# Layer end of a two-layer encoder: gate rows in other PSUM banks, x update on VectorE, mean square from scaled squares

## Chip, core and metric

The kernel runs on one core of a Trainium2 chip, in one launch. The metric is the device time of that launch in microseconds (us), the median of several runs. Five engines work side by side, each through its own list of instructions in order: TensorE (PE), VectorE (DVE), ScalarE (ACT), GpSimd (POOL) and SyncE (SP), which issues nearly all DMAs.

## The reference

Two encoder layers over 512 tokens of width 1024, in float32. Each layer normalises x, modulates it by the conditioning vector c, runs three token mixers side by side, merges them by sigmoid gates, projects, normalises again and adds the result to x:

```python
for l in range(DEPTH):                                   # DEPTH = 2
    mod = c_act @ w_ada[l] + b_ada[l]
    shift, scale, gate = split_cols(mod, (D, D, D))
    h = rms_norm(x, g_pre[l]) * (1.0 + scale) + shift
    ...                                                  # projections h @ w_in[l]
    o_a = (mla_branch(...) * silu(za)) @ w_o_mla[l]
    o_b = (swa_branch(...) * silu(zb)) @ w_o_swa[l]
    o_c = (diff_branch(...) * silu(zc)) @ w_o_diff[l]
    g = sigmoid(gcols)
    y = (g[0] * o_a + g[1] * o_b + g[2] * o_c) @ w_out[l]
    x = x + gate * rms_norm(y, g_post[l])

def rms_norm(x, g):
    return x * rsqrt(mean(x * x) + EPS) * g
```

The change concerns the last line and the rms_norm at the head of the next layer.

## The kernel before

Every float32 matmul is split in three: both operands are cut into a high part and a low part, and high x high, low x high and high x low are summed in PSUM (mm3, lines 87 to 89). A weight comes by DMA into one of two "wr" buffers, ScalarE makes the high part (L81), VectorE the low part (L84). The 512 tokens are four blocks of 128, t = 0 to 3.

Tiles are taken from pools by tag, each tag with a fixed number of buffers used in turn; a new tile waits until the last reader of the old one is done. PSUM has 8 banks of 128x512: "dn" has 2 (projections, merge outputs, out projection), "sc" 2 (attention scores), "tr" 2 (transposes), "pj" and "av" one each. In SBUF "tf" has 2 buffers, "x5" 2 (bias tiles of the attention; the profile names them x), "big" 8. A scheduler sets the order of each engine's instructions at build time from its own estimate of times; at run time each engine keeps that order.

A layer ends in three steps.

1. gate_rows (called in rest_of_layer, after the last gate projections and before the merge of the third mixer). The vector `gate` before its bias is a sum over the 128 partitions of acc; a matmul with ones sums and spreads it to all partitions (L292, L293). VectorE adds the bias row b_ada (L298) and multiplies by g_post (L299); both rows are loaded by DMAs issued in the same function (L295, L297). This is done for two halves of 512 columns. Then merge multiplies the third mixer by its weights, 8 output blocks of 12 matmuls in "dn" banks, each evicted by VectorE (L548).

2. out_phase. The first half of the out projection goes into four banks (acc4); its squares are summed by ScalarE (L1019) and it is multiplied by gg[0] (L1020). The second half is done token block by token block in "dn" banks: 24 matmuls, a Square with a sum (L1036), the sum of the two sums (L1038), the mean with epsilon (L307), the power -0.5 on GpSimd (L309), the multiply by gg[1] (L1041). x is loaded by SP (L1028), and the update is x + rs * y: in the first half of blocks 0 to 2 by two instructions of GpSimd (L1045, L1047), elsewhere by one of VectorE (L1049). SP stores the result (L1051).

3. Between the layers boundary_tok takes each updated block on: a Square of x with a sum on ScalarE (L315 in normed), mean (L307), power (L309), scaling (L317), eight transposes on TensorE (L371), modulation by four VectorE (L375) and four ScalarE (L379) instructions, and the split into hTh and hTl. The first projections of layer 1 (mla_in_step, "sc" banks for t = 0 and 1) read these.

Of the kernel before, what the change touches and what calls it, by code (L numbers as in the profile page):

```python
# [13 lines left out]
AF = mybir.ActivationFunctionType  # L14
ALU = mybir.AluOpType
AX = mybir.AxisListType

P = 128
S = 512
D = 1024  # L20
# [30 lines left out]
def hybrid_kernel(ctx, tc, x, c, w_ada, b_ada, g_pre, g_post, w_in, g_q, w_uq, g_kv, w_ukv,  # L51
# [16 lines left out]
    def stat(n):  # L68
        return T("st", [P, n], F32, 24)
# [3 lines left out]
    def Q(tag):  # L73
        count[0] += 1
        return ps.tile([P, S], F32, tag=tag, name=f"ps_{tag}_{count[0]}", bufs=PB[tag])
# [204 lines left out]
    def gate_rows(l):  # L280
        bg_step(100)
        acc = gate_acc[0]
        gg = []
        for hf in range(2):
            lo = hf * S
            g = T("x5", [P, 896])
            pg = Q("dn")
            ah = T("pt", [P, S], F32R)
            al = T("pt", [P, S], F32R)
            act_copy(ah, acc[:, lo:lo + S])  # L290
            sub(al, acc[:, lo:lo + S], f(ah))
            pe.matmul(pg, onesr, ah, start=True, stop=False)  # L292
            pe.matmul(pg, onesr, al, start=False, stop=True)  # L293
            bb = T("tf", [P, S])
            sp.dma_start(out=bb, in_=b_ada[l:l + 1, 2 * D + lo:2 * D + lo + S].broadcast_to([P, S]))  # L295
            gp = T("tf", [P, S])
            sp.dma_start(out=gp, in_=g_post[l:l + 1, lo:lo + S].broadcast_to([P, S]))  # L297
            dve.tensor_tensor(out=g[:, :S], in0=pg, in1=bb, op=ALU.add)  # L298
            dve.tensor_tensor(out=g[:, :S], in0=g[:, :S], in1=gp, op=ALU.mult)  # L299
            gg.append(g[:, :S])  # L300
        return gg

    def rms_cols(ssq, n, cols):
# [5 lines left out]
        pool.tensor_tensor(out=rs, in0=ms, in1=mhalf[:, 0:cols], op=ALU.pow)  # L309
        return rs  # L310

    def normed(xt):
        xn = T("big", [P, D])
        ssq = stat(1)
        act.activation(out=xn, in_=xt, func=AF.Square, accum_out=ssq)  # L315
        rs = rms_cols(ssq, [D], 1)
        dve.tensor_scalar(out=xn, in0=xt, scalar1=rs[:, 0:1], scalar2=None, op0=ALU.mult)  # L317
        return xn

# [684 lines left out]
    def out_phase(l, mm, gg, nhh, nhl):  # L1004
        us = out_half(l, 0, mm)
        acc = acc4(True)
        for k in range(KT):
            wh, wl = us[k // 2]
            cs_ = slice((k % 2) * S, (k % 2) * S + S)
            for t in range(NT):  # L1010
                ts_ = slice(t * P, (t + 1) * P)
                mm3(acc[t], mm[k][0][:, ts_], mm[k][1][:, ts_], wh[:, cs_], wl[:, cs_],
                    k == 0, k == KT - 1)
        ys = []
        for t in range(NT):
            y = T("zz", [P, S])
            ssq = stat(2)
            jk = T("tf", [P, S])
            act.activation(out=jk, in_=acc[t], func=AF.Square, accum_out=ssq[:, 0:1])  # L1019
            dve.tensor_tensor(out=y, in0=acc[t], in1=gg[0], op=ALU.mult)  # L1020
            ys.append((y, ssq))
        us = out_half(l, 1, mm)
        ws = list(mla_in_weights(l + 1)) if nhh is not None else None
        for t in range(NT):
            ts_ = slice(t * P, (t + 1) * P)
            y, ssq = ys[t]
            xt = T("big", [P, D])
            sp.dma_start(out=xt, in_=xin[l][t * P:(t + 1) * P, :])  # L1028
            a = Q("dn")
            for k in range(KT):  # L1030
                wh, wl = us[k // 2]
                cs_ = slice((k % 2) * S, (k % 2) * S + S)
                mm3(a, mm[k][0][:, ts_], mm[k][1][:, ts_], wh[:, cs_], wl[:, cs_],
                    k == 0, k == KT - 1)
            jk = T("tf", [P, S])
            act.activation(out=jk, in_=a, func=AF.Square, accum_out=ssq[:, 1:2])  # L1036
            tot = stat(1)
            dve.tensor_tensor(out=tot, in0=ssq[:, 0:1], in1=ssq[:, 1:2], op=ALU.add)  # L1038
            rs = rms_cols(tot, [D], 1)
            jk = T("tf", [P, S])  # L1040
            dve.tensor_tensor(out=jk, in0=a, in1=gg[1], op=ALU.mult)  # L1041
            for hf, yh in enumerate((y, jk)):
                xh = xt[:, hf * S:(hf + 1) * S]
                if hf == 0 and t < 3:
                    pool.tensor_scalar(out=yh, in0=yh, scalar1=rs, scalar2=1.0, op0=ALU.mult,  # L1045
                                       op1=ALU.mult)
                    pool.tensor_tensor(out=xh, in0=xh, in1=yh, op=ALU.add)  # L1047
                else:
                    dve.scalar_tensor_tensor(out=xh, in0=yh, scalar=rs, in1=xh, op0=ALU.mult,  # L1049
                                             op1=ALU.add)  # L1050
                sp.dma_start(out=xout[l][t * P:(t + 1) * P, hf * S:(hf + 1) * S], in_=xh)  # L1051
            if nhh is not None:
                ends = boundary_tok(l + 1, t, xt, nhh, nhl)
                if t == NT - 1:
                    fence[:] = ends
        return ws
# [142 lines left out]
```

## Time and profile before

| | |
|---|---|
| time, median of 3 runs | 1209.92 us (1208.97 to 1210.29) |
| the profiled execution, its own time | 1208.57 us |
| its span, first to last instruction | 1206.8 us |
| PE matmuls busy | 1165.8 us (97%) |
| DVE busy | 840.5 us (70%) |
| ACT busy | 632.2 us (52%) |
| POOL busy | 194.7 us (16%) |
| mean granted TensorE clock | 0.993 of full speed |

The profile is of one execution. Busy time is the time in which an engine had an instruction in work; matmuls are pipelined, so the next one starts before the one before it has ended, and their durations overlap. Idle time of the other engines costs nothing as long as TensorE does not wait for them. In a timeline the bracket behind an instruction gives the idle time of its engine ahead of it and what ended that; where an instruction waits for several things, the profile names the one that came last by its records. Times within the span are counted from its start.

### The profile page before, as it was taken

The numbers are of one execution on the slowest core, as the hardware profiler recorded it, in microseconds if no ns is written. First come the engines' busy times: TensorE is split into PE (matmuls) and PEld (weight loads), VectorE is DVE, ScalarE is ACT, GpSimd is POOL, SyncE is SP. The second block draws the span as 40 slices with busy tenths as digits, with TensorE's granted clock in tenths as the row PEclk, the third lists the DMA queues.
The fourth block names the chain that finished last, engine by engine and source line by source line (L and its number), as shares of the span: only waits on it lengthen the run. The fifth ranks groups of instructions, "written<-read, shape, count | busy, mean of one in ns | idle before, by whom it ended". The sixth has DMA issues, their size and how long they took to land.

```text
span 1206.8 us, 15578 instructions
## 1 busy us (share of the span) xinstructions
PE 1165.8 (97%) x5428; PEld 946.0 (78%) x5428; DVE 840.5 (70%) x1748; ACT 632.2 (52%) x1250; POOL 194.7 (16%) x238
## 2 busy tenths in 40 slices
PE   5799999999999999999999999999999999999997
PEld 4777788778887888887878888888888888888786
DVE  7854776988865687765557567678785468776553
ACT  5453565655543457654347456565554345665432
POOL 3410211111210010101141001122121001010123
PEclk9899999999999999999999999999999999999999
DMA  9638522356356333343454432324532432333442
GB/s 316 205 98 250 147 77 73 91 132 182 105 146 163 98 81 83 105 115 120 144 171 127 119 105 72 84 53 124 147 101 83 105 92 81 86 105 97 139 159 85
DMA packets 169523, 146.86 MB, mean 122 GB/s; under 512 B 7679, under 2 KB 146999, under 8 KB 169444
## 3 DMA queue, kind: packets, MB, share of 16 engines
q1 hardware_dynamic: 169316, 145.85, 41.9%
q8 instruction: 43, 0.70, 0.3%
q14 instruction: 36, 0.29, 0.1%
q0 software_dynamic: 128, 0.01, 0.0%
HBM read 135.83 MB, written 14.20 MB: 124 GB/s over the span
## 4 chain that ended last, share of the span: by engine, by line
PE 79%; DMA 7%; DVE 7%; issue 2%; POOL 2%; ACT 2%; SPq 1%; DVEq 0%; POOLq 0%; ACTq 0%
PE ps_dn L87 18%; PE ps_dn L89 18%; PE ps_dn L88 18%; PE ps_tr L691 5%; DMA wr<-in_w_in 3%; PE ps_sc L87 2%; PE ps_sc L89 2%; PE ps_sc L88 2%; PE ps_av L700 1%; PE ps_av L701 1%; PE ps_sc L939 1%; PE ps_sc L940 1%; DVE wl L84 1%; DMA wr<-in_w_ada 1%; PE ps_pj L87 1%
## 5 line engine op out<-in xcount | busy, mean ns | idle before, releaser
L87 PE MATMUL ps_dn<-hTh,wh 128*128 128x512 f32 x840 | 336.2, 400 | 1.7 <-ACT tf L479 1.1
L89 PE MATMUL ps_dn<-hTh,wl 128*128 128x512 f32 x840 | 334.5, 398 | 0.5 <-DVE wl L84 0.5
L88 PE MATMUL ps_dn<-hTl,wh 128*128 128x512 f32 x840 | 334.4, 398 | 0.0
L84 DVE TENSOR_TENSOR wl<-wr,wh 128x1024 fp32r<-128x1024 f32 x141 | 178.9, 1269 | 120.0 <-ACT wh L81 119.3
L81 ACT ACTIVATE wh<-wr 128x1024 fp32r<-128x1024 f32 x141 | 149.1, 1058 | 178.9 <-PE ps_dn L88 95.9
L87 PEld LDWEIGHTS ps_dn<-hTh,wh 128*128 128x128 f32 x840 | 158.1, 188 | 37.8 <-ACT tf L479 1.6
L89 PEld LDWEIGHTS ps_dn<-hTh,wl 128*128 128x128 f32 x840 | 157.9, 188 | 37.4 <-DVE wl L84 0.9
L88 PEld LDWEIGHTS ps_dn<-hTl,wh 128*128 128x128 f32 x840 | 158.0, 188 | 35.6
L84 DVE TENSOR_TENSOR pt<-ps_tr,pt 128x512 fp32r<-128x512 f32 x136 | 92.2, 684 | 35.2 <-ACT pt L81 34.4
L81 ACT ACTIVATE pt<-ps_tr 128x512 fp32r<-128x512 f32 x136 | 78.7, 596 | 70.8 <-PE ps_tr L691 69.5
L762 POOL TENSOR_SCALAR p<-p,st 128x512 f32<-128x512 f32 x64 | 48.6, 778 | 291.1 <-DVE st L760 237.6
L691 PE MATMUL ps_tr<-ident,p 128*128 128x128 f32 x544 | 93.0, 273 | 0.8 <-POOL p L762 0.8
L691 PEld LDWEIGHTS ps_tr<-ident,p 128*128 128x128 f32 x544 | 70.1, 141 | 20.7 <-POOL p L762 1.4
L87 PE MATMUL ps_dn<-u,wh 128*128 128x512 f32 x192 | 77.0, 401 | 1.3 <-DVE x L298 1.3
L950 POOL TENSOR_SCALAR ta<-ta,st 128x512 f32<-128x512 f32 x32 | 26.6, 833 | 313.9 <-DVE st L949 197.5
L89 PE MATMUL ps_dn<-u,wl 128*128 128x512 f32 x192 | 76.8, 400 | 0.0
L88 PE MATMUL ps_dn<-u,wh 128*128 128x512 f32 x192 | 76.1, 396 | 0.0
L881 POOL TENSOR_SCALAR p<-p,st 128x256 f32<-128x256 f32 (+1 forms) x64 | 41.4, 665 | 161.9 <-DVE st L879 116.0
L758 ACT ACTIVATE p<-ps_sc,st 128x512 f32<-128x512 f32 x64 | 43.7, 685 | 36.1 <-DVE st L757 35.9
L757 DVE TENSOR_REDUCE st<-ps_sc 128x1 f32<-128x512 f32 x64 | 43.3, 685 | 15.9 <-PE ps_sc L89 15.4
L873 ACT ACTIVATE p<-p,st 128x256 f32<-128x256 f32 (+1 forms) x64 | 35.6, 556 | 20.9 <-DVE st L871 20.2
L87 PEld LDWEIGHTS ps_dn<-u,wh 128*128 128x128 f32 x192 | 36.1, 188 | 10.4 <-DVE x L298 2.2
(345 smaller groups left out, 2105.0 us busy)
## 6 DMA issues: line engine op xcount, KB each, us to landing
wr<-in_w_in SPq DMA_DIRECT2D x105, 512.0 KB, 3.9
wr<-in_w_ada SPq DMA_DIRECT2D x32, 512.0 KB, 3.6
wr<-in_w_out SPq DMA_DIRECT2D x16, 512.0 KB, 3.7
big<-in_w_ada SPq DMA_DIRECT2D x10, 512.0 KB, 9.3
big<-in_x SPq DMA_DIRECT2D x8, 512.0 KB, 5.1
wr<-in_w_o_mla SPq DMA_DIRECT2D x8, 512.0 KB, 3.7
wr<-in_w_o_swa SPq DMA_DIRECT2D x8, 512.0 KB, 3.6
wr<-in_w_o_diff SPq DMA_DIRECT2D x8, 512.0 KB, 3.5
```

The lines of the kernel that those rows point to most:

```text
L81: return act.activation(out=out_, in_=in_, func=AF.Copy, scale=scale)
L84: return (eng or dve).tensor_tensor(out=out_, in0=a, in1=b, op=ALU.subtract)
L87: pe.matmul(o, ah, bh, start=start, stop=False)
L88: pe.matmul(o, ah, bl, start=False, stop=False)
L89: pe.matmul(o, al, bh, start=False, stop=stop)
L691: pe.transpose(tr[:, i * P:(i + 1) * P], b, ident)
L757: dve.tensor_reduce(out=nm[:, t:t + 1], in_=s, axis=AX.X, op=ALU.max, negate=True)
L758: act.activation(out=pr[:, t], in_=s, func=AF.Exp, bias=nm[:, t:t + 1], accum_out=sm[:, t:t + 1])
L762: pool.tensor_scalar(out=pr[:, t], in0=pr[:, t], scalar1=rr[:, t:t + 1], scalar2=1.0, op0=ALU.mult, op1=ALU.mult)
L873: act.activation(out=pr[:, i, :w], in_=pr[:, i, :w], func=AF.Exp, bias=nm[:, i:i + 1], accum_out=sm[:, i:i + 1])
L881: pool.tensor_scalar(out=pr[:, i, :w], in0=pr[:, i, :w], scalar1=rr[:, i:i + 1], scalar2=1.0, op0=ALU.mult, op1=ALU.mult)
L950: pool.tensor_scalar(out=pc[1], in0=pc[1], scalar1=rr[:, 1:2], scalar2=1.0, op0=ALU.mult, op1=ALU.mult)
```

## The change

In gate_rows the row sums go into "sc" banks instead of "dn" banks; the bias row is loaded straight into the tile that will hold the result, and both loads stand ahead of the matmuls in the code. In out_phase and normed the Square takes a scale of 1/sqrt(1024), so that its sum is the mean square; epsilon is added to the first half's mean right after it (L1027 of the changed kernel), and the sum of both halves is one instruction that reads this as a scalar (rms_of). The x update of all blocks and halves is on VectorE (L1052). rms_cols stays for the other norms.

```diff
--- before.py
+++ after.py
@@ -284,18 +284,18 @@
         for hf in range(2):
             lo = hf * S
             g = T("x5", [P, 896])
-            pg = Q("dn")
+            sp.dma_start(out=g[:, :S], in_=b_ada[l:l + 1, 2 * D + lo:2 * D + lo + S]
+                         .broadcast_to([P, S]))
+            gp = T("tf", [P, S])
+            sp.dma_start(out=gp, in_=g_post[l:l + 1, lo:lo + S].broadcast_to([P, S]))
+            pg = Q("sc")
             ah = T("pt", [P, S], F32R)
             al = T("pt", [P, S], F32R)
             act_copy(ah, acc[:, lo:lo + S])
             sub(al, acc[:, lo:lo + S], f(ah))
             pe.matmul(pg, onesr, ah, start=True, stop=False)
             pe.matmul(pg, onesr, al, start=False, stop=True)
-            bb = T("tf", [P, S])
-            sp.dma_start(out=bb, in_=b_ada[l:l + 1, 2 * D + lo:2 * D + lo + S].broadcast_to([P, S]))
-            gp = T("tf", [P, S])
-            sp.dma_start(out=gp, in_=g_post[l:l + 1, lo:lo + S].broadcast_to([P, S]))
-            dve.tensor_tensor(out=g[:, :S], in0=pg, in1=bb, op=ALU.add)
+            dve.tensor_tensor(out=g[:, :S], in0=pg, in1=g[:, :S], op=ALU.add)
             dve.tensor_tensor(out=g[:, :S], in0=g[:, :S], in1=gp, op=ALU.mult)
             gg.append(g[:, :S])
         return gg
@@ -309,11 +309,17 @@
         pool.tensor_tensor(out=rs, in0=ms, in1=mhalf[:, 0:cols], op=ALU.pow)
         return rs
 
+    def rms_of(ms, eps):
+        me, rs = stat(1), stat(1)
+        dve.tensor_scalar(out=me, in0=ms, scalar1=eps, scalar2=None, op0=ALU.add)
+        pool.tensor_tensor(out=rs, in0=me, in1=mhalf[:, 0:1], op=ALU.pow)
+        return rs
+
     def normed(xt):
         xn = T("big", [P, D])
-        ssq = stat(1)
-        act.activation(out=xn, in_=xt, func=AF.Square, accum_out=ssq)
-        rs = rms_cols(ssq, [D], 1)
+        ms = stat(1)
+        act.activation(out=xn, in_=xt, func=AF.Square, scale=D ** -0.5, accum_out=ms)
+        rs = rms_of(ms, EPS)
         dve.tensor_scalar(out=xn, in0=xt, scalar1=rs[:, 0:1], scalar2=None, op0=ALU.mult)
         return xn
 
@@ -1014,16 +1020,19 @@
         ys = []
         for t in range(NT):
             y = T("zz", [P, S])
-            ssq = stat(2)
+            ms = stat(2)
             jk = T("tf", [P, S])
-            act.activation(out=jk, in_=acc[t], func=AF.Square, accum_out=ssq[:, 0:1])
+            act.activation(out=jk, in_=acc[t], func=AF.Square, scale=D ** -0.5,
+                           accum_out=ms[:, 0:1])
+            dve.tensor_scalar(out=ms[:, 0:1], in0=ms[:, 0:1], scalar1=EPS, scalar2=None,
+                              op0=ALU.add)
             dve.tensor_tensor(out=y, in0=acc[t], in1=gg[0], op=ALU.mult)
-            ys.append((y, ssq))
+            ys.append((y, ms))
         us = out_half(l, 1, mm)
         ws = list(mla_in_weights(l + 1)) if nhh is not None else None
         for t in range(NT):
             ts_ = slice(t * P, (t + 1) * P)
-            y, ssq = ys[t]
+            y, ms = ys[t]
             xt = T("big", [P, D])
             sp.dma_start(out=xt, in_=xin[l][t * P:(t + 1) * P, :])
             a = Q("dn")
@@ -1033,21 +1042,15 @@
                 mm3(a, mm[k][0][:, ts_], mm[k][1][:, ts_], wh[:, cs_], wl[:, cs_],
                     k == 0, k == KT - 1)
             jk = T("tf", [P, S])
-            act.activation(out=jk, in_=a, func=AF.Square, accum_out=ssq[:, 1:2])
-            tot = stat(1)
-            dve.tensor_tensor(out=tot, in0=ssq[:, 0:1], in1=ssq[:, 1:2], op=ALU.add)
-            rs = rms_cols(tot, [D], 1)
+            act.activation(out=jk, in_=a, func=AF.Square, scale=D ** -0.5,
+                           accum_out=ms[:, 1:2])
+            rs = rms_of(ms[:, 1:2], ms[:, 0:1])
             jk = T("tf", [P, S])
             dve.tensor_tensor(out=jk, in0=a, in1=gg[1], op=ALU.mult)
             for hf, yh in enumerate((y, jk)):
                 xh = xt[:, hf * S:(hf + 1) * S]
-                if hf == 0 and t < 3:
-                    pool.tensor_scalar(out=yh, in0=yh, scalar1=rs, scalar2=1.0, op0=ALU.mult,
-                                       op1=ALU.mult)
-                    pool.tensor_tensor(out=xh, in0=xh, in1=yh, op=ALU.add)
-                else:
-                    dve.scalar_tensor_tensor(out=xh, in0=yh, scalar=rs, in1=xh, op0=ALU.mult,
-                                             op1=ALU.add)
+                dve.scalar_tensor_tensor(out=xh, in0=yh, scalar=rs, in1=xh, op0=ALU.mult,
+                                         op1=ALU.add)
                 sp.dma_start(out=xout[l][t * P:(t + 1) * P, hf * S:(hf + 1) * S], in_=xh)
             if nhh is not None:
                 ends = boundary_tok(l + 1, t, xt, nhh, nhl)
```

The instruction lists differ from those of before only at the layer ends. In the rows below a number behind a name tells tiles of one tag apart; lines below the first edit have moved by 3 to 9 (L548 is L554 now, L1041 is L1049).

VectorE in the gate rows of layer 0, x being the tiles of the two halves and wl the low parts of merge weights. Before:

```order
L298 TENSOR_TENSOR x_1186_5281<-ps_dn_5282,tf_5289 128x512
L84 TENSOR_TENSOR wl_5404<-wr_5402,wh_5403 128x1024
L299 TENSOR_TENSOR x_1186_5281<-x_1186_5281,tf_5291 128x512
L298 TENSOR_TENSOR x_1192_5295<-ps_dn_5296,tf_5303 128x512
L548 SCALAR_TENSOR_TENSOR p_5183<-p_5183,ps_dn_5317 128x512
L299 TENSOR_TENSOR x_1192_5295<-x_1192_5295,tf_5305 128x512
L548 SCALAR_TENSOR_TENSOR p_5183<-p_5183,ps_dn_5336 128x512
L553 SCALAR_TENSOR_TENSOR op_5316<-p_5183,op_5315 128x512
```

Now:

```order
L298 TENSOR_TENSOR x_1186_5281<-ps_sc_5285,x_1186_5281 128x512
L298 TENSOR_TENSOR x_1191_5294<-ps_sc_5298,x_1191_5294 128x512
L84 TENSOR_TENSOR wl_5402<-wr_5400,wh_5401 128x1024
L299 TENSOR_TENSOR x_1186_5281<-x_1186_5281,tf_5283 128x512
L299 TENSOR_TENSOR x_1191_5294<-x_1191_5294,tf_5296 128x512
L554 SCALAR_TENSOR_TENSOR p_5183<-p_5183,ps_dn_5315 128x512
L554 SCALAR_TENSOR_TENSOR p_5183<-p_5183,ps_dn_5334 128x512
L84 TENSOR_TENSOR wl_5446<-wr_5444,wh_5445 128x1024
```

The second L298 has come up from behind L299 to stand right after the first, ahead of the low part, and both L299 stand together; the two merge evictions (L548, now L554) follow each other.

VectorE at the layer boundary, from the first token block's second half on; st are statistics of one column, big the x block and its normalised copy, zz the first half of y. Before:

```order
L1038 TENSOR_TENSOR st_5723<-st_5617 128x1
L1041 TENSOR_TENSOR tf_5729<-ps_dn_5696,x_1192_5295 128x512
L307 TENSOR_SCALAR st_5725<-st_5723 128x1
L1049 SCALAR_TENSOR_TENSOR big_5694<-tf_5729,st_5726,big_5694 128x512
L307 TENSOR_SCALAR st_5739<-st_5737 128x1
L1038 TENSOR_TENSOR st_5797<-st_5622 128x1
L1041 TENSOR_TENSOR tf_5803<-ps_dn_5770,x_1192_5295 128x512
L317 TENSOR_SCALAR big_5736<-big_5694,st_5740 128x1024
```

Now:

```order
L314 TENSOR_SCALAR st_5725<-st_5615 128x1
L1049 TENSOR_TENSOR tf_5729<-ps_dn_5698,x_1191_5294 128x512
L1052 SCALAR_TENSOR_TENSOR big_5696<-zz_5614,st_5726,big_5696 128x512
L1052 SCALAR_TENSOR_TENSOR big_5696<-tf_5729,st_5726,big_5696 128x512
L314 TENSOR_SCALAR st_5738<-st_5736 128x1
L323 TENSOR_SCALAR big_5735<-big_5696,st_5739 128x1024
L314 TENSOR_SCALAR st_5796<-st_5621 128x1
L1049 TENSOR_TENSOR tf_5800<-ps_dn_5769,x_1191_5294 128x512
```

The input of the power (L307, now L314) stands ahead of the multiply by gg[1], and L1038 is gone; two updates of x stand where one was.

SP in layer 0, where the diff moves the bias loads; tf<-gb and p<-gc are gates computed early and read back, wr are weights. Before:

```order
L110 DMA wr_4923<-in_w_in 128x8x128
L110 DMA wr_5043<-in_w_o_swa 128x4x256
L528 DMA tf_4744<-gb_2_1879 128x512
L110 DMA wr_5081<-in_w_in 128x8x128
L528 DMA tf_4956<-gb_3_1914 128x512
L110 DMA wr_5114<-in_w_o_swa 128x4x256
L528 DMA tf_5041<-gb_4_1949 128x512
L509 DMA p_5183<-gc_3_2024 128x512
L110 DMA wr_5135<-in_w_in 128x8x128
L110 DMA wr_5184<-in_w_in 128x8x128
```

Now:

```order
L110 DMA wr_4923<-in_w_in 128x8x128
L110 DMA wr_5043<-in_w_o_swa 128x4x256
L287 DMA x_1186_5281<-in_b_ada 128x512
L534 DMA tf_4744<-gb_2_1879 128x512
L110 DMA wr_5081<-in_w_in 128x8x128
L534 DMA tf_4956<-gb_3_1914 128x512
L110 DMA wr_5114<-in_w_o_swa 128x4x256
L534 DMA tf_5041<-gb_4_1949 128x512
L515 DMA p_5183<-gc_3_2024 128x512
L110 DMA wr_5135<-in_w_in 128x8x128
```

The first bias row is loaded ahead of three of the gate rows that are read back; it came behind all of these before.

## Rows read from the trace of the kernel before

**Rows 1.** Part 1 of the page: engine, busy us (share of the span), instructions.

```profile
PE 1165.8 (97%) x5428; PEld 946.0 (78%) x5428; DVE 840.5 (70%) x1748; ACT 632.2 (52%) x1250; POOL 194.7 (16%) x238
```

**Rows 2.** Timeline, TensorE, 555 to 561: start, duration, engine, line, instruction, [idle before <-releaser].

```profile
555.07 0.39 PE L292 MATMUL ps_dn<-pt,onesr 128*128 128x512 f32 x1
555.30 0.39 PE L293 MATMUL ps_dn<-pt,onesr 128*128 128x512 f32 x1
556.47 0.51 PE L292 MATMUL ps_dn<-pt,onesr 128*128 128x512 f32 x1 [0.78 <-DVE x L298]
556.81 0.39 PE L293 MATMUL ps_dn<-pt,onesr 128*128 128x512 f32 x1
...
560.38 0.50 PE L87 MATMUL ps_dn<-u,wh 128*128 128x512 f32 x1 [0.38 <-DVE x L298]
```

**Rows 3.** Timeline, TensorE, gate rows of layer 1.

```profile
1131.57 0.51 PE L292 MATMUL ps_dn<-pt,onesr 128*128 128x512 f32 x1 [0.78 <-DVE x L298]
...
1136.05 0.50 PE L87 MATMUL ps_dn<-u,wh 128*128 128x512 f32 x1 [0.95 <-DVE x L298]
```

**Rows 4.** Timeline, VectorE, gate rows and merge of layer 0.

```profile
559.63 0.69 DVE L298 TENSOR_TENSOR x<-ps_dn,tf 128x512 f32<-128x512 f32 x1 [1.49 <-DMA tf<-in_b_ada]
...
566.93 0.68 DVE L548 SCALAR_TENSOR_TENSOR p<-p,ps_dn 128x512 f32<-128x512 f32 x1
```

**Rows 5.** Timeline, DMA issues of SP before and in the gate rows.

```profile
538.52 0.34 SPq L297 DMA_DIRECT2D tf<-in_g_post  x1
...
556.44 0.34 SPq L295 DMA_DIRECT2D tf<-in_b_ada  x1
```

**Rows 6.** Timeline, ScalarE, at the same place.

```profile
556.00 0.58 ACT L512 ACTIVATE p<-ps_dn 128x512 f32<-128x512 f32 x1
```

**Rows 7.** Timeline, TensorE, boundary of the layers.

```profile
626.71 1.09 PE L371 MATMUL ps_tr<-ident,big 128*128 128x128 f32 x8 [1.40 <-DVE st L307]
...
633.64 0.45 PE L87 MATMUL ps_sc<-u,hTh 128*128 128x416 f32 x1 [1.37 <-ACT hTh L81]
```

**Rows 8.** Timeline, ScalarE, Squares of x at the boundary.

```profile
615.61 1.06 ACT L315 ACTIVATE big<-big 128x1024 f32<-128x1024 f32 x1 [4.24 <-POOL big L1047]
...
622.20 1.06 ACT L315 ACTIVATE big<-big 128x1024 f32<-128x1024 f32 x1 [4.86 <-POOL big L1047]
...
630.53 1.06 ACT L315 ACTIVATE big<-big 128x1024 f32<-128x1024 f32 x1 [2.78 <-POOL big L1047]
```

**Rows 9.** Timeline, VectorE, end of the kernel.

```profile
1200.92 0.16 DVE L1038 TENSOR_TENSOR st<-st 128x1 f32<-128x1 f32 x1 [3.31 <-ACT tf L1036]
...
1201.60 0.14 DVE L307 TENSOR_SCALAR st<-st 128x1 f32<-128x1 f32 x1
```

**Rows 10.** Timeline, VectorE, last readers of the bias tiles of heads 2 and 3.

```profile
480.99 0.68 DVE L941 CUSTOM_DVE_ANT_0 ta<-ps_sc,x 128x512 f32<-128x512 f32 x1
...
513.03 0.68 DVE L941 CUSTOM_DVE_ANT_0 ta<-ps_sc,x 128x512 f32<-128x512 f32 x1
```

**Rows 11.** Timeline, GpSimd, boundary.

```profile
612.30 0.56 POOL L309 TENSOR_TENSOR st<-st,mhalf 128x1 f32<-128x1 f32 x1 [27.00 <-DVE st L307]
...
614.28 1.29 POOL L1047 TENSOR_TENSOR big<-big,zz 128x512 f32<-128x512 f32 x1
...
626.79 0.99 POOL L309 TENSOR_TENSOR st<-st,mhalf 128x1 f32<-128x1 f32 x1 [2.63 <-DVE st L307]
```

**Rows 12.** Timeline, VectorE, boundary.

```profile
612.08 0.14 DVE L307 TENSOR_SCALAR st<-st 128x1 f32<-128x1 f32 x1
612.89 0.75 DVE L1049 SCALAR_TENSOR_TENSOR big<-tf,st,big 128x512 f32<-128x512 f32 x1 [0.67 <-POOL st L309]
...
619.56 0.75 DVE L1049 SCALAR_TENSOR_TENSOR big<-tf,st,big 128x512 f32<-128x512 f32 x1 [0.71 <-POOL st L309]
...
626.68 1.29 DVE L84 TENSOR_TENSOR hTl<-ta,hTh 128x512 fp32r<-128x512 f32 x2
```

**Rows 13.** Timeline, DMA issue of SP, x of token block 1.

```profile
615.99 0.42 SPq L1028 DMA_DIRECT2D big<-in_x  x1
```

## Prediction

> **What bounds the kernel now.** I read the page's busy table first: TensorE's matmuls cover 97% of the span [rows 1], so only a stretch where TensorE stands still can give time back, and a change to the other engines counts by the waits that it ends there. Then I listed TensorE's waits (I name its row only where a number hangs on it) and opened the timeline at each one that the diff could touch. There are three places.
>
> Gate rows, layer 0: matmul starts are 0.23 us apart when nothing is in the way (555.07 to 555.30), then 1.17 to the next one, and 0.34 after it, since the first matmul after a gap is slow [rows 2]. So a wait costs the bracketed idle time plus 0.16 (1.17 - 0.23 = 0.94 against the 0.78 shown), plus 0.10 for the slow restart. A second wait of 0.38 follows at 560.38. Layer 1 has the same pair, 0.78 and 0.95 [rows 3]. The profile names L298 for all four. For the second of each pair that is right: L298 of half 1 waited for its bias row [rows 4], which SP could issue only at 556.44 [rows 5], when L298 of half 0 had given up the "tf" buffer. For the first, the matmul needs the "dn" bank of the last gate projection, and its reader is ScalarE's L512, which ran from 556.00 behind a weight conversion [rows 6]; L298 may have come late as well, and either way the bank is the cause.
>
> Boundary of layers 0 and 1: two waits, 1.40 for the transposes of token block 1 (t=1) and 1.37 for its hTh [rows 7]. ScalarE's rows tell why: three times its Square of x (L315) stood 4.24, 4.86 and 2.78 us idle for GpSimd's L1047 [rows 8], with other evictions queued behind it.
>
> Tail: after the last matmul the end waits for one chain, ScalarE, VectorE, GpSimd's power, VectorE, store [rows 9].
>
> **The change part by part.** *Gate rows.* The four row sums write "sc" banks, last read by the scores of the differential heads, whose last reader ended at 513.71 [rows 10], 41 us earlier; so no matmul waits for a bank. The merge outputs then follow the gate projections in the "dn" banks: the one that needs L512's last bank, free at 556.58 [rows 6], is the second, and it starts at 556.0 + 12 x 0.23 = 558.8. The bias rows go straight into the "x" tiles. These are free at 481.67 and 513.71 [rows 10]; SP has both loads in its order about there, so they wait for next to nothing. The g_post rows take the two "tf" buffers that L295 and L297 got before, the later one at 538.52 [rows 5], 17 us ahead. All four waits of rows 2 and 3 go. Layer 0: 0.94 + 0.54 + 2 x 0.10 = 1.68. Layer 1: 0.94 + 1.11 + 0.20 = 2.25.
>
> What is late next here: VectorE now runs both L298 before a weight's low part (merge blocks 4 and 5), 0.69 of delay for something wanted 11 us later. Tightest is the eviction of merge block 2, whose bank block 4 needs. Before, it ran from 566.93 to 567.61 [rows 4], and block 4 could start at 560.38 + 0.1 + 36 x 0.233 = 568.9: 1.3 to spare. What stands ahead of it hangs on the end of block 1, which moves with TensorE, and in the new order the same three instructions stand there, two of them exchanged. So about 1.3 stays; I take no cost, and 0 to 0.7 per layer (one instruction more ahead of it than I think, plus its wait) as bounds, a gain being excluded where nothing waits.
>
> *x update on VectorE, boundary.* I keep the old clock and look at what each step gains. Before, for t=0: L307 at 612.08, the power from 612.30 to 612.86, then two GpSimd passes until 614.28 + 1.29 = 615.57 [rows 11, 12]. After, the sum of two squares is folded into the power's input, and that instruction stands ahead of the 0.61 us multiply instead of behind it: 0.68 sooner (the step from 1200.92 to 1201.60 in [rows 9] is the same one). So the power starts at 611.62, the first update 0.59 later (612.30 to 612.89, [rows 11, 12]) at 612.21, and both are done 2 x 0.75 later [rows 12] at 613.7: 1.9 sooner than GpSimd's 615.57, and the Square of x with them.
> For t=1 a new wait decides: its x row block is loaded by SP behind the stores of t=0. Before, that load was issued at 615.99, 0.42 after GpSimd's end, and used at 619.56 [rows 12, 13], so it takes 3.57 at most. Now: 613.7 + 0.42 + 3.57 = 617.7, two updates, done at 619.2. Before, the Square of t=1 started at 622.20 [rows 8]; now 3.0 sooner. What follows it is no longer than before, so the transposes are ready by 626.71 - 3.0 = 623.7. TensorE is there at 625.15 (626.71 - 1.56): the wait goes, worth 1.40 + 0.16 = 1.56.
> For t=2: load at 619.6, there at 623.2, x done at 624.7, against 630.5 [rows 8]; its Square of 1.06 ends at 625.8 and no longer holds up t=1's eviction on ScalarE. Before, that eviction took 633.64 - 630.53 - 1.06 = 2.05 from the Square's end to the matmul [rows 7, 8]. Now it starts with the transposes done at 625.15 + 0.8 = 625.95, with one half-width Square (under 1.06) of t=3 in between: 629.1 at the latest. The projection wants it at 633.64 - 1.52 - 1.56 = 630.6. The second wait goes too, with 1.5 left: 1.37 + 0.15 = 1.52. With 0.1 for a restart the boundary gives 3.2. Bounds: 0, if the loads of x come as late as GpSimd's results did, and 3.2, all that is idle there.
> VectorE pays for this: per layer 3 more updates of 0.75, four additions of epsilon (0.14, as L307) against four L1038 of 0.16, about 2.2 us. They fall into time in which VectorE waited: 0.67 and 0.71 for a power before each update [rows 12], and for GpSimd's x after it. Without that cover each block would be 0.75 later, half of the margins above.
>
> *Squares.* A scale of 1/32 inside the Square changes no count; nearest are the Squares without it. I cost it at zero. The same edit in the input stage of layer 0 keeps every engine's order, also zero.
>
> *Tail.* The fold brings the power forward by 0.68 and the multiply by gg[1] runs beside it: 0.69 long, as L298, against 0.22 + 0.59 = 0.81 from the power's input to the first update [rows 11, 12]. Gain 0.68. The one price that no row shows is that of a power beside this multiply. Bounds: 0.56 alone, and 0.99 as at 626.79 beside a VectorE subtraction whose inputs both lie in SBUF [rows 11, 12]. I take 0.56, since the multiply reads one of its inputs from PSUM; with 0.99 the tail gives 0.25.
> The Trainium skill speaks to this in "SBUF — State Buffer", section "Who interferes with whom": a VectorE instruction with two SBUF inputs and a GpSimd one that reads SBUF shut each other out for a whole instruction, one with a single SBUF input does not. The row of 0.99 agrees with its first half; of the second no row here shows a full overlap. By the rule the tail gives 0.68 and the sum stands; without it, by the row's 0.99, the sum is 7.4.
>
> **Sum.** 1.68 + 3.2 + 2.25 + 0.68 = 7.8 us. Between 640 and 1120 TensorE has no wait listed at all, so what layer 0 gains is carried through layer 1 unless loads pace it. The profiled execution took 1208.57 with a span of 1206.8, so 1200.8; the runs' median is 1.35 above it: 1209.92 - 7.8 = 1202.1.
>
> **The rivals.** *The boundary keeps its waits.* For: a chain of store, load, update per block (0.42 + 3.57 + 1.5 = 5.5) is as long as TensorE's 24 matmuls for a block (24 x 0.23 = 5.5), and VectorE's new order puts the updates ahead of evictions. Against: margins of about 1.5, and a load of 3.57 is an upper bound. Left are gates and tail: 4.6, 1205.3.
> *The gate rows keep theirs in another form* (the low parts or merge evictions behind both L298). For: a margin of 1.3 only. Left are boundary and tail: 3.9, 1206.0.
> *Layer 1 gives it back*: its weights arrive just in time and pace TensorE. For: SP waits for buffers all along. Against: those buffers are freed by engines that follow TensorE. Left: 2.25 + 0.68 = 2.9, 1207.0; if the tail's store takes its part as well, no change that can be told.
> *Slower: the bias row blocks SP.* SP issues in order. If the first bias load gets the buffer of head 3 and not of head 2, SP stands from 481.7 to 513.7 [rows 10] with all weights behind it. Three converted weights of 24 x 0.23 = 5.6 us cover 17 us, 15 are lost per layer: 1202.1 + 30 = 1232. It decides from the point where the buffer comes more than those 17 us late. Against: two buffers in turn, and head 2's tile is the older.
>
> **How the numbers follow.** Chances: forecast 0.70, boundary kept 0.14, gates kept 0.06, given back 0.06 (half of it as no change), slower 0.04. The range goes from 1201.0 (1.1 under the forecast: the runs spread over 1.3, and shorter queues on VectorE might give a little more) to 1205.9 (the boundary rival with half a microsecond of spread). 0.2% is 2.4 us, about what a measurement of this kernel can tell from no change; faster by more than that 0.88, within it 0.08, slower 0.04.
>
> **What would show it.** Right: no TensorE idle time before the row sums, the second merge output or the transposes after the out projection; L298 twice in a row on VectorE; the Square of x released by VectorE at intervals near 5.5 us; GpSimd with only its powers at both layer ends; 0.7 us less from the last matmul to the end. Wrong: an SP gap near 482, a wait of TensorE for a low part near 567, transposes waiting for a load of x, or powers of 1 us in the tail.

## The result and the profile after

The changed kernel takes 1202.84 us (median of 6 runs, 1201.53 to 1203.88) against 1210.34 for the kernel before (6 runs beside it). The ratio is 0.9937, 95% interval 0.9926 to 0.9947, so 6.4 to 9.0 us less. The forecast was 1202.1. Its profiled execution has a span of 1201.1 us. Part 1 of its page, which answers to [rows 1], with GpSimd 17 us less busy and VectorE 3 more:

```profile
PE 1167.7 (97%) x5428; PEld 948.0 (79%) x5428; DVE 843.8 (70%) x1754; ACT 632.2 (53%) x1250; POOL 177.8 (15%) x226
```

To see where the time went I took five matmuls that stand at the same place of both programs, and compared the stretches between their starts. Timeline of TensorE in the kernel before: a matmul well ahead of the gate rows of layer 0, the first of the out projection's second half, the first of layer 1's next projection, the counterpart of the first in layer 1, and the last of all.

```profile
458.39 0.48 PE L970 MATMUL ps_pj<-pt,onesr 128*128 128x512 f32 x1
...
602.12 0.39 PE L87 MATMUL ps_dn<-big,op 128*128 128x512 f32 x1
...
649.15 0.39 PE L87 MATMUL ps_dn<-hTh,wh 128*128 128x512 f32 x1
...
1033.49 0.48 PE L970 MATMUL ps_pj<-pt,onesr 128*128 128x512 f32 x1
...
1199.71 0.40 PE L89 MATMUL ps_dn<-wh,pt 128*128 128x512 f32 x1
```

The same five in the changed kernel:

```profile
459.53 0.48 PE L976 MATMUL ps_pj<-pt,onesr 128*128 128x512 f32 x1
...
601.58 0.39 PE L87 MATMUL ps_dn<-big,op 128*128 128x512 f32 x1
...
646.29 0.39 PE L87 MATMUL ps_dn<-hTh,wh 128*128 128x512 f32 x1
...
1030.66 0.48 PE L976 MATMUL ps_pj<-pt,onesr 128*128 128x512 f32 x1
...
1194.62 0.40 PE L89 MATMUL ps_dn<-wh,pt 128*128 128x512 f32 x1
```

The first is 1.14 us later than before; then 142.05 us instead of 143.73 pass to the second, so the gate rows of layer 0 gave 1.68. The table has this for every stretch and for the profiled run of every experiment below (us, minus is shorter than the kernel before). The boundary column runs from the second of the five matmuls to the third; the tail is what is left of the span after the last one starts.

| kernel | first 458 us | gate rows, layer 0 | boundary | layer 1 to its gates | gate rows, layer 1 | tail |
|---|---|---|---|---|---|---|
| forecast | 0 | -1.68 | -3.2 | 0 | -2.25 | -0.68 |
| changed | +1.14 | -1.68 | -2.32 | +0.03 | -2.26 | -0.61 |
| a1_again, the changed one once more | -0.13 | -1.69 | -2.06 | +0.02 | -2.25 | -0.59 |
| p1_gates, gate rows alone | +1.28 | -1.68 | -0.23 | +0.02 | -2.25 | -0.04 |
| p2_update, x update alone | +1.35 | +0.18 | -1.87 | +0.03 | -0.12 | +0.03 |
| p3_squares, squares and fold alone | +0.68 | +0.40 | +1.77 | 0 | +0.02 | -0.67 |
| g1_bank, other banks alone | +1.09 | -1.72 | -0.08 | +0.03 | -1.34 | +0.02 |
| g2_bias, early bias rows alone | +1.50 | -0.68 | +0.33 | +0.03 | -0.86 | -0.02 |
| n1_nofold, changed without squares | +1.95 | -1.68 | -1.88 | 0 | -2.25 | -0.04 |
| r1_xahead, changed, x loaded ahead | +0.24 | -1.68 | -3.27 | +0.03 | -2.25 | -0.67 |
| r2_xahead, the same once more | +3.15 | -1.68 | -3.27 | +0.03 | -2.25 | -0.58 |
| n2_pool_xahead, GpSimd and x ahead | +1.94 | -1.68 | -1.27 | 0 | -2.25 | -0.64 |
| n3_nofold_xahead, no squares, x ahead | +0.23 | -1.68 | -3.22 | 0 | -2.25 | +0.02 |

Where a stretch is unchanged, the last five columns differ by up to 0.5 us, mostly in the sizes of its waits; the first differs by up to 3.3 with next to nothing changed in it. (In p2_update, g1_bank and g2_bias some 0.4 us of the column "gate rows, layer 1" is lost after the merge, spread evenly over the matmuls, which start 232 ns apart against 230 in the others; why stays open. Without it these cells read -0.5, -1.7 and -1.3.)

*Gate rows of layer 0.* Timeline of TensorE in the changed kernel, answering to [rows 2]: row sums and merge follow each other 0.23 us apart, no bracket is left.

```profile
555.98 0.40 PE L89 MATMUL ps_dn<-hTh,wl 128*128 128x512 f32 x1
556.21 0.39 PE L296 MATMUL ps_sc<-pt,onesr 128*128 128x512 f32 x1
...
556.91 0.39 PE L297 MATMUL ps_sc<-pt,onesr 128*128 128x512 f32 x1
557.14 0.39 PE L87 MATMUL ps_dn<-u,wh 128*128 128x512 f32 x1
```

*Boundary.* TensorE has one listed wait here, where [rows 7] had two: the transposes of t=2 for VectorE's scaling. (The second trace of this kernel, a1_again, has two, 0.18 and 0.21.)

```profile
630.52 1.09 PE L377 MATMUL ps_tr<-ident,big 128*128 128x128 f32 x8 [0.24 <-DVE big L323]
```

Timeline of VectorE in the same stretch (the update of x is L1052, the scaling L323):

```profile
616.34 0.68 DVE L1049 TENSOR_TENSOR tf<-ps_dn,x 128x512 f32<-128x512 f32 x1
618.93 0.75 DVE L1052 SCALAR_TENSOR_TENSOR big<-zz,st,big 128x512 f32<-128x512 f32 x1 [1.92 <-DMA big<-in_x]
619.60 0.75 DVE L1052 SCALAR_TENSOR_TENSOR big<-tf,st,big 128x512 f32<-128x512 f32 x1
...
623.05 1.36 DVE L381 TENSOR_SCALAR ta<-ps_tr,amul,ashf 128x128 f32<-128x128 f32 x4
...
625.11 0.69 DVE L84 TENSOR_TENSOR hTl<-ta,hTh 128x512 fp32r<-128x512 f32 x1
625.72 0.75 DVE L1052 SCALAR_TENSOR_TENSOR big<-zz,st,big 128x512 f32<-128x512 f32 x1
626.38 0.75 DVE L1052 SCALAR_TENSOR_TENSOR big<-tf,st,big 128x512 f32<-128x512 f32 x1
...
628.43 1.37 DVE L381 TENSOR_SCALAR ta<-ps_tr,amul,ashf 128x128 f32<-128x128 f32 x4
629.71 0.75 DVE L323 TENSOR_SCALAR big<-big,st 128x1024 f32<-128x1024 f32 x1
```

For t=1 it stood 1.92 us for the load of x. DMA issues of SP there, answering to [rows 13] (two weights, two stores, the load):

```profile
608.14 3.53 SPq L110 DMA_DIRECT2D wr<-in_w_in  x2
612.87 1.00 SPq L1054 DMA_DIRECT2D x1d<-big  x2
613.92 0.42 SPq L1037 DMA_DIRECT2D big<-in_x  x1
```

*Tail.* The power runs beside the multiply L1049 and takes 0.55; the chain of [rows 9] has lost one step. VectorE and GpSimd:

```profile
1195.84 0.21 DVE L314 TENSOR_SCALAR st<-st 128x1 f32<-128x1 f32 x1 [3.25 <-ACT tf L1045]
1195.97 0.68 DVE L1049 TENSOR_TENSOR tf<-ps_dn,x 128x512 f32<-128x512 f32 x1
1196.13 0.55 POOL L315 TENSOR_TENSOR st<-st,mhalf 128x1 f32<-128x1 f32 x1 [4.99 <-DVE st L314]
1196.71 0.75 DVE L1052 SCALAR_TENSOR_TENSOR big<-zz,st,big 128x512 f32<-128x512 f32 x1
```

### The profile page after: what moved, and what is told of

It is laid out like the page before. It is cut to its first block, busy times and chain, and to the rows that moved or that the text cites. A ratio compares the mean times of both kernels' runs of the same rounds, so it can differ in the third digit from the quotient of the medians.

```text
span 1201.1 us, 15565 instructions
## 1 busy us (share of the span) xinstructions
PE 1167.7 (97%) x5428; PEld 948.0 (79%) x5428; DVE 843.8 (70%) x1754; ACT 632.2 (53%) x1250; POOL 177.8 (15%) x226
## 4 chain that ended last, share of the span: by engine, by line
PE 81%; DVE 8%; DMA 6%; issue 2%; ACT 1%; SPq 1%; POOL 1%; DVEq 0%; POOLq 0%; ACTq 0%
PE ps_dn L87 19%; PE ps_dn L88 19%; PE ps_dn L89 19%; PE ps_tr L697 5%; DMA wr<-in_w_in 2%; DVE o L202 2%; PE ps_sc L89 2%; PE ps_sc L87 2%; PE ps_sc L88 2%; PE ps_av L706 1%; PE ps_av L707 1%; PE ps_sc L945 1%; PE ps_sc L946 1%; PE ps_pj L87 1%; PE ps_pj L89 1%
## 5 line engine op out<-in xcount | busy, mean ns | idle before, releaser
L952 ACT ACTIVATE p<-p,st 128x512 f32<-128x512 f32 x32 | 23.1, 723 | 37.9 <-DVE st L950 37.8
```

## The experiments

The theory to test was the prediction's division of the gain; the open question was why the boundary gave 2.3 us (2.06 in the second trace) and not 3.2. All ratios are to the kernel before, run on the same chip.

**Gate rows alone (p1_gates).** The first hunk of the change put into the kernel before:

```diff
-            pg = Q("dn")
+            sp.dma_start(out=g[:, :S], in_=b_ada[...])
+            gp = T("tf", [P, S]); sp.dma_start(out=gp, in_=g_post[...])
+            pg = Q("sc")
...
-            dve.tensor_tensor(out=g[:, :S], in0=pg, in1=bb, op=ALU.add)
+            dve.tensor_tensor(out=g[:, :S], in0=pg, in1=g[:, :S], op=ALU.add)
```

> The kernel before with the new gate rows alone (score banks, bias rows ahead). Theory: the two pairs of waits at the gate rows go in both layers and nothing else moves: 1.7 us in layer 0 and 2.25 in layer 1, so 3.9 us less, ratio 0.9967; the waits of 1.40 and 1.37 at the layer boundary stay as they are. Rival, that layer 1 is paced by its weights and returns what layer 0 gains: 2.25 less, ratio 0.998.

Measured: 1205.68, ratio 0.9972 (0.9961 to 0.9983). The trace gives 1.68 and 2.25, and both waits stay at the boundary, 1.17 and 1.32 us. This part stands by itself, and layer 1 gives nothing back.

**Banks alone (g1_bank), bias rows alone (g2_bias).** The two halves of that hunk. g1_bank has this line only, g2_bias all the others:

```diff
-            pg = Q("dn")
+            pg = Q("sc")
```

> The kernel before with one edit: the four row sums write score banks; the bias rows are loaded as late as before, so the second addition of each pair still waits for its row. Theory A: a bank is the cause of both waits of each pair (of the first the bank of the last gate projection, of the second the bank that the late addition holds), so with the row sums elsewhere all four waits go although VectorE still stands for the bias row: 3.9 us, ratio 0.9967, as with both edits. Theory B, as the prediction divided it: the second wait is the bias row's, and VectorE's stand delays the eviction of the merge: only the first wait of each pair goes, 2 x 0.94 = 1.9 us, ratio 0.9984.

> The kernel before with the other half: bias rows loaded ahead into the result tiles, row sums in the banks of the projections as before. Both theories: the first wait of each pair (0.78 us, the bank of the last gate projection) stays. The second goes, since the addition no longer holds its bank for the late row: 0.54 + 1.11 + 0.2 = 1.85 us, ratio 0.9985. Rival, that the bank of the first addition is still late for the merge: a second wait of some tenths stays, 1 us, ratio 0.999.

g1_bank: 1206.62, ratio 0.9980 (0.9971 to 0.9988). In layer 0 both waits go (1.72). In layer 1 they go too, but VectorE's stands for the bias row (1.59 us) and then for g_post (1.86) make an eviction of the merge late. VectorE and then TensorE there:

```profile
1134.17 0.69 DVE L298 TENSOR_TENSOR x<-ps_sc,tf 128x512 f32<-128x512 f32 x1 [1.59 <-DMA tf<-in_b_ada]
```

```profile
1142.08 0.50 PE L87 MATMUL ps_dn<-u,wh 128*128 128x512 f32 x1 [0.30 <-DVE p L548]
```

So by the trace theory A holds for the four waits named, and of theory B that much is true: the late row comes back as another, smaller wait, and the early rows are worth their place in layer 1. The time alone would not show it: 0.9980 lies nearer to B's 0.9984, and its interval leaves out A's 0.9967, since the new wait and the 0.4 us after the merge take back a part.

g2_bias: 1208.20, ratio 0.9991 (0.9982 to 1.0000); the interval holds both the 0.9985 and the rival's 0.999. In the trace the first wait of each pair stays at 0.78 and the second goes, for 0.68 us in layer 0 and 1.3 in layer 1 (0.86 with the loss after the merge); no smaller wait is left in its place, so the rival falls. TensorE in layer 0:

```profile
557.97 0.50 PE L296 MATMUL ps_dn<-pt,onesr 128*128 128x512 f32 x1 [0.78 <-DVE x L298]
```

**x update alone (p2_update).**

```diff
-                if hf == 0 and t < 3:
-                    pool.tensor_scalar(out=yh, ...)
-                    pool.tensor_tensor(out=xh, ...)
-                else:
+                dve.scalar_tensor_tensor(out=xh, in0=yh, scalar=rs, in1=xh, ...)
```

> The kernel before with the x update of all blocks on VectorE alone; squares, power and gate rows as before. Theory: GpSimd's two passes are the larger part of what delays x at the boundary, but without the fold each power comes 0.68 us later than in the changed kernel, which shows as a longer wait of the transposes of t=2: 0.24 + 0.7 = 0.9 us. The boundary then gives 2.3 - 0.7 = 1.6 us, the tail nothing: ratio 0.9987. Rival, that the fold has no part in the boundary: 2.3 us, ratio 0.998. Rival, that GpSimd is not the cause: 0.

Measured: 1207.73, ratio 0.9990 (0.9981 to 0.9998); the boundary gave 1.87. Both waits of [rows 7] are gone, and one of 0.25 came up at hTh of a later block, not at the transposes of t=2, where the theory had put it:

```profile
643.83 0.46 PE L87 MATMUL ps_av<-u,hTh 128*128 128x416 f32 x1 [0.25 <-ACT hTh L81]
```

The size lies between the theory's 1.6 and the rival's 2.3; GpSimd as the main cause is borne out.

**Squares and fold alone (p3_squares).** The edit in out_phase; the Square in normed gets the same scale:

```diff
-            act.activation(out=jk, in_=a, func=AF.Square, accum_out=ssq[:, 1:2])
-            ...
-            rs = rms_cols(tot, [D], 1)
+            act.activation(out=jk, in_=a, func=AF.Square, scale=D ** -0.5, accum_out=ms[:, 1:2])
+            rs = rms_of(ms[:, 1:2], ms[:, 0:1])
```

> The kernel before with the scaled squares and the folded sum alone; x is still updated by GpSimd in three half blocks, the gate rows are as before. Theory: the tail gives 0.6 us; at the boundary the powers come 0.68 us sooner in each of blocks 0 to 2, which adds up from block to block since each Square of x holds up the next eviction, so that the waits of 1.40 and 1.37 shrink together by 1.4 to 2.0 us: 2.0 to 2.6 us in all, ratio 0.998. Rival, that only the move off GpSimd ends the waits: the tail alone, 0.6 us, ratio 0.9995, and waits within 0.3 us of 1.40 and 1.37.

Measured: 1210.45, ratio 1.0010 (1.0000 to 1.0020). Both expectations fell: the tail gave its 0.67, but the boundary got 1.77 longer. Timeline of TensorE there:

```profile
634.00 0.45 PE L87 MATMUL ps_sc<-u,hTh 128*128 128x416 f32 x1 [2.19 <-ACT hTh L81]
...
636.34 0.71 PE L89 MATMUL ps_sc<-u,hTl 128*128 128x416 f32 x1 [0.82 <-DVE hTl L84]
636.85 0.55 PE L87 MATMUL ps_sc<-u,hTh 128*128 128x416 f32 x1
```

The wait of the transposes is gone, but TensorE reaches hTh of t=1 earlier and waits there. GpSimd still holds x of t=2: its first pass stretched to 2.21 us in that block (1.20 and 0.69 in the two before), the Square followed at 630.31, and ScalarE's order now had another Square ahead of t=1's eviction. As the second of these waits ended, at 636.34, the granted clock fell to the 1.2 GHz level. Table of stretches: length, busy us of PE, PEld, DVE, ACT and POOL (instructions), granted clock as a share of 2.4 GHz, DMA share, GB/s:

```profile
634.00:636.00 2.00, 1.52 (x10) 1.20 (x10) 2.00 (x4) 0.76 (x2) 0.00 (x0) 1.00 0.06 23
636.00:638.00 2.00, 1.66 (x5) 1.61 (x6) 1.99 (x7) 1.88 (x5) 0.55 (x1) 0.59 0.64 240
638.00:640.00 2.00, 2.00 (x8) 1.94 (x7) 1.97 (x5) 1.54 (x4) 0.00 (x0) 0.55 0.00 0
```

Some ten matmuls at 0.345 instead of 0.187 us apart make 1.6 us, nearly all of the loss; the waits themselves (3.0 against 2.8) hardly differ. This is read from one trace, and no run takes the clock by itself. The twelve times of this kernel lie between 1206.47 and 1212.51, so whether the clock falls there in every run is not shown.

**Changed without the squares (n1_nofold).**

```diff
-            rs = rms_of(ms[:, 1:2], ms[:, 0:1])
...
+            dve.tensor_tensor(out=tot, in0=ssq[:, 0:1], in1=ssq[:, 1:2], op=ALU.add)
+            rs = rms_cols(tot, [D], 1)
```

> The changed kernel without the squares: the new gate rows and the x update on VectorE, but the Square unscaled and the sum of both halves and the mean in two instructions as before. Theory: the parts add where they do not meet: gate rows 1.7 and 2.25, boundary 1.9 as with the update alone, tail 0: 5.8 us, ratio 0.9952. The fold is then worth 0.2 to 0.4 us at the boundary and 0.6 in the tail once VectorE updates x, though alone, with GpSimd, it cost 1.7. Rival, that the fold costs at the boundary here too: the boundary gives 3 us or more.

Measured: 1203.91, ratio 0.9956 (0.9939 to 0.9972); the trace gives 1.68, 1.88, 2.25 and nothing in the tail, the theory's 5.8. The fold, harmful alone, gives 0.6 in the tail once GpSimd is out of the way. Its 0.2 to 0.4 at the boundary are hardly more than the 0.26 by which the two traces of the changed kernel differ there.

**x loaded a block ahead (r1_xahead, r2_xahead, beside a1_again).**

```diff
+        def load_x(t):
...
+        load_x(0)
         for t in range(NT):
-            xt = T("big", [P, D])
-            sp.dma_start(out=xt, in_=xin[l][t * P:(t + 1) * P, :])
+            xt = xts[t]
+            if t + 1 < NT:
+                load_x(t + 1)
```

> The changed kernel with x of block t+1 loaded before the work of block t is issued, so that its load no longer stands behind the stores of block t. Theory: what the boundary lost against the forecast (2.3 us gained instead of 3.2) is the chain of store, load and update, in which the load of t=1 took 5.0 us and not 3.6; with the load ahead, the first update of t=1 follows its power within 0.2 us, the transposes of t=2 do not wait, and 0.4 to 0.9 us goes: ratio to the kernel before 0.993, against 0.9937 for the changed kernel. Rival, that VectorE's queue (modulations and low parts ahead of the update and the scaling of t=2) sets it: the wait of 0.24 us stays and the time is that of the changed kernel.

> The changed kernel with x loaded a block ahead, once more, for a comparison with the changed kernel in the same session. From the trace of the first run of it the boundary gave 3.2 us and not 2.3, so 0.9 us less than the changed kernel: ratio to the kernel before 0.9930 against 0.9937. Rival, that the difference does not reach the end of the program: the same ratio.

> The changed kernel once more, beside the next one on the same chip. Its own ratio is expected at 0.9937 as before; its trace is to show whether the 1.1 us by which the first 530 us of the changed kernel's profiled run were longer belongs to the change (then it shows again) or to the run (then that stretch differs by under 0.6 us or has the other sign).

Measured: r1_xahead 1201.39, ratio 0.9941 (0.9929 to 0.9952); r2_xahead 1201.03, ratio 0.9932 (0.9918 to 0.9945), beside a1_again with 1201.99, ratio 0.9944 (0.9931 to 0.9956). Both traces show the boundary at 3.27, 1.0 to 1.2 us more than the changed kernel's two: a little above the theory's 0.4 to 0.9, and the forecast's 3.2. TensorE waits for nothing between 598 and 660. x of t=1 was loaded with that of t=0, and its update follows the multiply at once, 2.9 us sooner than in the changed kernel, whose out projection began its second half 0.9 later (timeline of VectorE, r1_xahead):

```profile
615.27 0.68 DVE L1057 TENSOR_TENSOR tf<-ps_dn,x 128x512 f32<-128x512 f32 x1
616.01 0.75 DVE L1060 SCALAR_TENSOR_TENSOR big<-zz,st,big 128x512 f32<-128x512 f32 x1
```

At the boundary this version beats both kernels. By the times it beats the kernel before, while against the changed one the intervals overlap, a microsecond being less than they resolve; and the span of r2_xahead's trace, 1202.2, is longer than that of a1_again, 1200.1, through its first 458 us alone. In a1_again the first 458 us are 0.13 shorter than before, not 1.14 longer: that part of the first trace belonged to the run.

**GpSimd against the late load (n2_pool_xahead); late powers with loads ahead (n3_nofold_xahead).** The first is r1_xahead with GpSimd's two passes put back, as below; the second is r1_xahead without the squares, by the edit of n1_nofold:

```diff
+                if hf == 0 and t < 3:
+                    pool.tensor_scalar(out=yh, in0=yh, scalar1=rs, scalar2=1.0, ...)
+                    pool.tensor_tensor(out=xh, in0=xh, in1=yh, op=ALU.add)
+                else:
```

> The changed kernel with x loaded a block ahead, but three half blocks of x updated by GpSimd as before. It tells GpSimd from the late load. Theory: GpSimd's two passes are the cause of the boundary's waits: with the loads ahead they still hold the Square of x of t=2 until some 5 us after its power's input, and TensorE waits 1.5 to 3 us in all at the boundary; against the kernel before the boundary gives 1 us at most, the sum is 4.5 to 5.5 us, ratio 0.996. Rival, that the load behind the stores was the cause all along: no wait at the boundary, 3.2 us there, 7.8 in all, ratio 0.9935.

> Gate rows and x update as in the changed kernel, x loaded a block ahead, squares as before. Theory: with the loads ahead there is enough room at the boundary that the later powers no longer show: no wait of TensorE from the out projection to layer 1, boundary 3.2 us, and only the tail's 0.6 us are missing: 7.1 us, ratio 0.9941. Rival, that the fold is needed there too: a wait of some tenths before the transposes of t=2 and 2.5 us at the boundary.

n2_pool_xahead: 1204.70, ratio 0.9962 (0.9949 to 0.9975); the boundary gives 1.27, a little more than allowed for, and two waits stay:

```profile
631.77 0.46 PE L87 MATMUL ps_sc<-u,hTh 128*128 128x416 f32 x1 [0.80 <-ACT hTh L81]
634.08 0.46 PE L89 MATMUL ps_sc<-u,hTl 128*128 128x416 f32 x1 [0.79 <-DVE hTl L84]
```

So the load was not the cause all along; with GpSimd's two passes back TensorE waits although x is there. n3_nofold_xahead: 1202.97, ratio 0.9950 (0.9935 to 0.9965); no wait at the boundary, 3.22 there, nothing in the tail. With the loads ahead the later powers no longer show at the boundary.

## Why the prediction was right, and where it was not

**Gate rows: right in mechanism and size.** 1.68 and 2.25 were forecast, 1.68 and 2.26 measured. The bank was the first wait (g2_bias leaves it, g1_bank removes it). The late row made the second by holding a bank, so either half of the edit removes it. What was to be late next did not come: the eviction of merge block 2 ran from 566.61 and its bank was wanted 48 matmuls after 557.14, at 568.3, so about 1.0 us was left of the 1.3 that was said. SP has no gap there that it did not have before: it issued the first bias row at 482.85, right behind a weight, so the slower rival never had its condition.

**Boundary: the cause right, the size too high by 0.9.** The step that failed was the bound on the load of t=1: "used at 619.56 [rows 12, 13], so it takes 3.57 at most". That was its time where little ran beside it. Tables of stretches, before and then changed (DMA share and GB/s are the last two columns):

```profile
614.50:615.50 1.00, 1.00 (x6) 0.80 (x5) 0.00 (x0) 0.00 (x0) 1.00 (x1) 1.00 0.87 315
615.50:616.50 1.00, 1.00 (x6) 0.80 (x5) 0.00 (x0) 0.89 (x1) 0.07 (x1) 1.00 0.07 27
```

```profile
613.00:614.00 1.00, 1.00 (x6) 0.82 (x5) 0.50 (x1) 0.47 (x1) 0.00 (x0) 1.00 1.05 310
614.00:615.00 1.00, 1.00 (x6) 0.77 (x5) 0.15 (x1) 1.00 (x3) 0.05 (x1) 1.00 1.11 386
615.00:616.00 1.00, 1.00 (x6) 0.83 (x5) 0.46 (x1) 0.26 (x2) 0.51 (x1) 1.00 1.26 336
```

Before, the weight was through and the first store all but through when the load was issued at 615.99, with only the second store beside it, and it landed in 3.5 us. In the changed kernel a weight comes at 611.31, both stores at 612.87 and 613.53 and the load at 613.92, and they are in the engines together; it landed in 4.9, and in 5.0 in the second trace. The DMA lists of the two traces, before and then changed:

```profile
big<-in_x SPq DMA_DIRECT2D x1, 512.0 KB, 3.5
```

```profile
big<-in_x SPq DMA_DIRECT2D x1, 512.0 KB, 4.9
```

So x of t=1 was done at 620.35, not 619.2 (on the old clock 0.5 later still). A second step failed behind it: for t=2 the prediction went from the load straight to the update and put VectorE's queue at nothing. The load was in time, but VectorE's own queue was not: the modulation L381 of t=0 and a low part stood ahead of its update, and L381 of t=1 ahead of its scaling, as the rows above show, so x came at 627.13 instead of 624.7. With the load ahead the stand for x and the wait of the transposes went and the forecast size appeared (3.27), which makes the load's place the cause by experiment. That edit also put a weight's load behind x of t=2 (613.39 in r1_xahead) and exchanged some matmuls; these were not tried apart, nor which of the three transfers the load lost its time to. The listed wait of 0.24 is only about half of the missing 0.9; the rest is not listed as waits, such as two matmuls 0.36 us apart at 635.90 where 0.19 is usual. The rival "boundary waits kept" named this chain and had a 14% chance; what came is about a quarter of it.

**GpSimd as the cause: right.** p2_update alone gives 1.87, and n2_pool_xahead keeps 1.6 us of waits.

**Layer 1 carries the gain on: right,** +0.03 between the two layer ends in the changed kernel, never more in any run.

**Tail: right,** 0.61 for 0.68. The multiply with one PSUM input left the power at 0.55. The missing 0.07 is L314, 0.21 with epsilon and mean as a scalar tile, where L307 took 0.14. The Trainium skill ("SBUF — State Buffer", section "Who interferes with whom") says that a VectorE instruction with at most one SBUF input, outside its 2-port modes, does not contend with GpSimd; this row, which the trace of before did not have, agrees. The prediction left out the condition on the modes.

**The sum.** The stages add to 6.87 us against 7.8. The medians differ by 7.5, and 6.87 lies within their interval of 6.4 to 9.0. The two spans differ by 5.7 only, since the profiled run of before had a short first 458 us; all but one of the twelve later traces lost 0.2 to 3.2 there. That the medians' gain came within 0.3 of the forecast, nearer than the stages, lies within their spread and is luck. The forecast of 1202.1 was 0.7 too low, 0.4 of it because the kernel before has a median of 1210.34 over six runs, not the 1209.92 of the three that the prediction started from. What the prediction did not see is that its parts don't add: the fold was costed as a gain wherever it stood, and alone, with GpSimd still updating x, the boundary became 1.77 longer in the one trace of it.

## What to carry over

A transfer's duration in a trace is a bound only for the traffic that ran beside it there (3.5 us before, 4.9 after, for the same load): if an edit issues it earlier, look at the DMA share of the stretch into which it moves, and load ahead of the stores if a buffer is free. When a chain has one slow producer, shortening another step of it (the fold) can move the wait to the next reader and not end it, as in p3_squares; remove the slow producer first. To tell a gain of 1 us in a program that varies by 3, compare the stretches between the same instructions of both traces, stage by stage.

## What the runs showed of the hardware

GpSimd's pass L1053 of one shape took 0.69, 1.20 and 2.21 us in p3_squares:

```profile
613.74 1.20 POOL L1053 TENSOR_SCALAR zz<-zz,st 128x512 f32<-128x512 f32 x1
...
619.96 0.69 POOL L1053 TENSOR_SCALAR zz<-zz,st 128x512 f32<-128x512 f32 x1
...
626.70 2.21 POOL L1053 TENSOR_SCALAR zz<-zz,st 128x512 f32<-128x512 f32 x1
```

In the 0.69 VectorE was idle; in the 1.20 an update of x (two SBUF inputs, 0.75) began with it; in the 2.21 three instructions with two SBUF inputs ran back to back from 626.49 to 628.43. In both slow cases the pass ended 0.48 after VectorE's last one. The section of the Trainium skill cited above says that the two shut each other out for a whole instruction, which fits.

A power on one column took 0.55 beside the multiply L1049, which reads one SBUF tile and PSUM, but 1.03 in r1_xahead and 1.02 in r2_xahead beside the scaling L323, which reads one SBUF tile and a column and writes an SBUF tile. VectorE and GpSimd in r1_xahead:

```profile
626.87 0.76 DVE L323 TENSOR_SCALAR big<-big,st 128x1024 f32<-128x1024 f32 x1
627.00 1.03 POOL L315 TENSOR_TENSOR st<-st,mhalf 128x1 f32<-128x1 f32 x1 [0.17 <-DVE st L314]
```

So having only one SBUF tile to read was not enough for VectorE to leave GpSimd alone here; whether L323 runs in one of the 2-port modes, which the sentence of the Trainium skill on one SBUF input excepts, no row says.

The granted clock fell to the 1.2 GHz level after waits of 2.19 and 0.82 us (p3_squares), but stayed at 2.4 GHz after 1.40 and 1.37 [rows 7] and after 0.80 and 0.79 (n2_pool_xahead).
